# A third seven-product group in the second layer's feed-forward part of a two-layer decoder trunk, with its weight-sum transfers placed in the first layer

## The chip, the cores and the metric

The kernel runs on one core of a Trainium2 chip. The metric is the time of one execution on the device in microseconds (us); of several executions the median is given. About 0.2% (1.6 us) is what a measurement of this kernel can tell from no change.

## The reference, cut to what matters

Two layers work on 256 tokens of 1024 features. Each ends with a SwiGLU feed-forward part, and the change concerns these two parts alone:

```python
D_MODEL = 1024; SEQ = 256
D_FF = 2816                       # ((8 * 1024 + 767) // 768) * 256
...
def swiglu(h, w_gu, w_down):
    g, u = jnp.split(h @ w_gu, 2, axis=-1)
    return (jax.nn.silu(g) * u) @ w_down
...
for l in range(DEPTH):            # DEPTH = 2
    ...                           # layer 0: gated convolution; layer 1: attention; both: memory attention
    x = x + swiglu(rms_norm(x, norm_ffn[l]), ffn_w_gu[l], ffn_w_down[l])
```

All inputs and outputs are float32.

## The kernel before, in words

**Products in two parts.** Every weight matrix streams from DRAM in chunks of 128 x 1024 floats (512 KB). `load_chunk` brings a chunk into a buffer `raw_...` with a DMA on the queue of SyncE (SP). ScalarE (ACT) rounds it into `hi_...` (`split_high`, a CAST), and VectorE (DVE) puts the remainder raw - hi into `lo_...` (`split_low`, a TENSOR_TENSOR). TensorE (PE) adds three products for each pair of parts (`mm3`), and the first of the three takes the lo part. So a weight is usable only when DMA, cast and subtraction are all done, in this order. There are five raw buffers (`RAWS`) and ten pairs of hi and lo (`WBUFS`): the DMA of chunk n can start only when the subtraction of chunk n - 5 is done.

**The feed-forward part** (`swiglu`). The 2816 hidden columns make eleven pairs `jp` of 256 columns. Pairs 0 and 1 are done in another way (`gate_up_rows`). An ordinary pair has two halves of 128 columns: `gate_up` multiplies the gate weights `wg` and the up weights `wu` into two PSUM tiles `gu`; ScalarE copies each out to `gu_sb` (COPY), VectorE adds, ScalarE applies SiLU (ACTIVATE), VectorE multiplies, and the product goes as hi and lo into `guT`. After each half stand two blocks of the down projection of the pair `jp - 2` (`down`, weights `wd`, accumulators `ff`). An ordinary pair with its down blocks streams six chunks: two `wg`, two `wu` and two `wd`.

**A group of seven products** (`seven`, `GROUPS`) replaces the gate and up products of two adjacent pairs jp and jp + 1. The tokens and features are cut in two halves each, the weights into four quarters B11, B12, B21, B22, and seven products (B11, B21, T1, T4, T2, B22, T3) of sums stand for eight. Three of them take quarters of the weights, four take sums of weights T1 to T4. The sums of activations (S1 to S4) are made on VectorE by `token_sums` at the start of the part, once for all groups of a layer. A group streams 14 chunks of weights and four of `wd`, 18 in all where two ordinary pairs stream 12, and it ends with eight transposes (`turn_parts4`, tile `pt_g`) on TensorE. Between the products stand eight down blocks.

**The sums of weights** are made by DMA alone, DRAM to DRAM (`sum_steps`): for each of T1 to T4 and each of two halves, a plain copy on SP's queue, and an adding transfer of another quarter on GpSimd's (POOL's) queue, 16 transfers of 512 KB for a group. T2 is begun from the finished T1, and T4 from the finished T2. `SUMS_AT` says by which chunk's load each transfer is issued: a hook at position n runs just before chunk n of the whole stream is loaded. Positions 64 to 135 are the chunks of the first layer's feed-forward part, 200 to 277 those of the second's.

**What sets the order.** The program is recorded in the order in which the Python code runs. A model clock (`Clock`, `note`) stands behind it: `Feed.pump`, polled after each matmul, issues the cast of the next chunk when the model says that the raw chunk has landed and ScalarE is free, and the subtraction likewise; `Feed.take` forces them at the latest when a product needs them. The model charges 1587 ns for a load, 1460 ns for a copy of `sum_steps` and 3300 ns for an adding transfer, one after the other. On the chip each engine then runs its instructions in just that order, whatever the time is.

The profile's line L464 is the matmul, L468 the transpose, L242 any VectorE or ScalarE operation, L481 a load, L553 and L551 a copy and an adding transfer of `sum_steps`. The first layer has one group, at pair 8, and the second layer two, at pairs 4 and 8.

Of the kernel before, what the change touches and what calls it, by code (L numbers as in the profile page):

```python
# [42 lines left out]
SPARE = 1500  # L43
LATER = 2000
BANKWISE = 5
GROUPS = ((8,), (4, 8))
SUMS_AT = ((44, 104, 104), (128, 220, 210))


class Rows:  # L50
# [18 lines left out]
def weight_plan():  # L69
# [38 lines left out]
    def seven_plan(l, jp):  # L108
        plan = []
        for name in SEVEN:  # L110
            if name[:4] == "down":
                plan += down_plan(l, jp - ROW_PAIRS + int(name[4]))
                continue
            for i in range(2):
                it = dict(name=f"w{name}_{l}_{jp}_{i}", a=2, b=2 * T, gain=None, pieces=1, halves=1)
                if name[0] == "T":
                    it["sum"] = l, jp, name, i
                else:
                    kh, part = QUARTER[name]
                    k, c = 4 * kh + 2 * i, part * DFF + jp * T  # L120
                    it["src"] = ffn_w_gu[l][k * P:(k + 2) * P, c:c + 2 * T]
                plan.append(it)
        return plan
# [7 lines left out]
    def ffn_plan(l):  # L131
        steps, last = ffn_steps()
        plan = []
        for kind, jp in steps + [("down", jp) for jp in last]:
            if kind == "gu" and jp in GROUPS[l]:
                plan += seven_plan(l, jp)
            elif kind == "gu" and jp - 1 in GROUPS[l] or kind == "down" and \
                    any(jp + ROW_PAIRS - g in (0, 1) for g in GROUPS[l]):
                pass
# [32 lines left out]
    for l in range(2):  # L172
        for jp in GROUPS[l]:
            for name in QUARTER:
# [224 lines left out]
def yoco_kernel(  # L399
# [22 lines left out]
    vector, scalar, pool = (Timed(clock, n, e) for n, e in  # L422
                            (("dve", nc.vector), ("act", nc.scalar), ("pool", nc.gpsimd)))
    side = Side(clock, tp=2, gu=2, half=HALVES, pair=PAIRS)
# [8 lines left out]
    def tp_tile(name):  # L433
        return ps_tp.tile([P, 4, P], F32, tag="tp", name=name)
# [21 lines left out]
    def tok(h):  # L456
        return slice(h * P, (h + 1) * P)
# [9 lines left out]
    def transpose(o, i):  # L467
        nc.tensor.transpose(o, i, ident[:i.shape[0], :i.shape[0]])  # L468
        clock.note("pe", 109, [o], [i], 200)
# [65 lines left out]
    def sum_steps(l, jp):  # L535
        for name in ("T1", "T2", "T3", "T4"):
            for i in range(2):
                weight_sums[l, jp, name, i] = aside.tile([P, 2, 2 * T], F32, name=f"{name}_{l}_{jp}_{i}")

        def step(name, source, i, add):  # L540
            dst = weight_sums[l, jp, name, i]
            if source[0] == "T":
                src = weight_sums[l, jp, source, i]
            else:
                n = quarters[l, jp, source, i]
                src = chunks[n * P:(n + 1) * P].rearrange("p (a n) -> p a n", a=2)

            def run():
                clock.free["dma"] = max(clock.free["dma"], clock.now)
                if add:  # L550
                    nc.gpsimd.dma_start(dst, src, accum_op=OP.add, max_dma_last_dim=2048)  # L551
                else:
                    nc.sync.dma_start(dst, src)  # L553
                clock.note("dma", 3300 if add else 1460, [], [])

            return run

        order = (("T1", "B11", False), ("T3", "B12", False), ("T1", "B12", True), ("T3", "B22", True),
                 ("T2", "T1", False), ("T2", "B22", True), ("T4", "T2", False), ("T4", "B21", True))
        return [step(name, source, i, add) for name, source, add in order for i in range(2)]  # L560

    plan, _, quarters, ffn_steps = weight_plan()
    feed = side.feed = Feed(clock, plan, load_chunk, split_high, split_low)
# [71 lines left out]
    def split_steps(hi, lo, pt, kind="tp"):  # L635
        scalar.copy(hi, pt)
        yield
        vector.tensor_sub(lo, pt, hi)
        side.give(kind)
        yield  # L640
# [398 lines left out]
        feed.hooks[36 + k] = [put_aside(k)]  # L1039

    for l in range(2):
        steps = [step for jp in GROUPS[l] for step in sum_steps(l, jp)]
        first, end, last = SUMS_AT[l]
        for n, step in enumerate(steps):
            at = min(first + (end - first) * n // len(steps), last + n - len(steps))
            feed.hooks.setdefault(at, []).append(step)


    def short_conv(act, into):
# [179 lines left out]
    def swiglu(l, src, done, fine_end=False, at_end=None):  # L1229
        act = src.act  # L1230
        guT = Act(side, [])

        def unit_of(j):
            if j // 4 == len(guT.units):
                guT.units.append(acts.tile([P, 4, 2, T], F32R, tag="unit", name=f"guT{l}_{j // 4}"))
            return guT.units[j // 4], j % 4
# [121 lines left out]
        def seven(jp):  # L1358

            u, j0 = unit_of(2 * jp)  # L1360
            bank_jobs, t = {}, {}
# [60 lines left out]
            def b22(acc):  # L1422
                side.finish(bank_jobs["T2"])
                yield from new("u0")
                vector.tensor_add(t["u0"], acc, t["m1"])
                side.give("gu")
                t["w used"] = True
                yield
                side.finish(bank_jobs["B21"])
                vector.tensor_mul(t["u0"], t["u0"], t["g0"])  # L1430
                side.give("half")
                yield spare(jp)
                yield from turn_parts4(t["u0"], 0)

            def t3(acc):
                while not t.get("w used"):
                    yield 0
                vector.tensor_add(t["m1"], acc, t["m1"])
                side.give("gu")
                yield  # L1440
                side.finish(bank_jobs["T4"])
                vector.tensor_sub(t["p5"], t["p5"], t["m1"])
                yield
                scalar.activation(t["p5"], t["p5"], AF.Silu)
                yield
                vector.tensor_mul(t["p5"], t["p5"], t["m1"])
                side.give("half")
                yield spare(jp)
                yield from turn_parts4(t["p5"], 1)
# [5 lines left out]
            def turn_parts4(src, h):  # L1455
                yield from side.hold("tp")
                pt = tp_tile("pt_g")
                for i in range(4):
                    transpose(pt[:, i, :], src[:, i * P:(i + 1) * P])
                side.give("half")  # L1460
                yield
                yield from split_steps(u[:, :, 0, tok(h)], u[:, :, 1, tok(h)], pt)

            EVICT = {"B11": b11, "B21": b21, "T1": t1, "T3": t3, "T2": t2, "B22": b22, "T4": t4}
            n = jp - ROW_PAIRS
# [17 lines left out]
                next_down()  # L1483
            next_down()
            for h, name in enumerate(("B22", "T3")):
                guT.add_job(h, jp // 2, bank_jobs[name])

        def down_w(jp):
            return [feed.take(f"wd{l}_{2 * jp + i}") for i in range(2)]
# [14 lines left out]
        steps, last = ffn_steps()  # L1504
        sums_job = [side.start(token_sums())]
        for jp in range(ROW_PAIRS, NP):
            if jp in GROUPS[l]:
                seven(jp)
            if jp in GROUPS[l] or jp - 1 in GROUPS[l]:
                continue  # L1510
            w = gu_w(jp)
            n = jp - ROW_PAIRS
            gate_up(jp, w, 0)
            wd = down_w(n) if ("down", n) in steps else None
            for h in range(2):
                if h == 1:
                    gate_up(jp, w, 1)
                for b in range(2 if wd else 0):
                    if h == b == 1:
                        feed.free(2)  # L1520
                    down(n, wd, h, b)
# [239 lines left out]
```

## Time and profile before

| | |
|---|---|
| median of three runs | 783.81 us (783.09 to 784.54) |
| the profiled execution, time | 783.19 us |
| its span, first to last instruction | 781.4 us |
| granted TensorE clock | 0.998 |
| TensorE busy | 773.5 us, 99% of the span |
| VectorE, ScalarE busy | 574.0 us (73%), 459.0 us (59%) |
| first layer's feed-forward part, on TensorE | 200.7 to 378.3 us |
| second layer's feed-forward part, on TensorE | 594.6 to 775.2 us |

The profiled execution lies 0.6 us under the median, inside the spread of the three runs. A busy TensorE is matmul after matmul without a pause; where it has to wait for a weight, the waiting shows as a hole between two of its rows. Each engine runs in order, so an instruction that waits holds back all that stand behind it.

### The profile page before, as it was taken

How to read it: one execution, taken by the hardware profiler on the slowest of the kernel's cores; microseconds unless marked ns; L12 is line 12 of the kernel's file. 1: busy time of each engine (PE TensorE's matmuls, PEld its weight loads, DVE VectorE, ACT ScalarE, POOL GpSimd, SP SyncE). 2: the span in 40 equal slices, each digit the busy share in tenths (PEclk: the TensorE clock that was granted, in tenths of full speed). 3: DMA queues.
4: the chain of work that ended last, by engine and by line, in shares of the span. 5: the costliest groups of instructions: out<-in, count | busy, mean ns of one | idle time of the engine just before them, and what ended most of it. 6: DMA issues, size and time to landing. Idle time of an engine off the chain costs nothing.

```text
span 781.4 us, 11230 instructions
## 1 busy us (share of the span) xinstructions
PE 773.5 (99%) x4147; PEld 664.8 (85%) x4147; DVE 574.0 (73%) x872; ACT 459.0 (59%) x728; POOL 39.1 (5%) x68
## 2 busy tenths in 40 slices
PE   9999999999999999999999999999999999999996
PEld 8988888898888888888888889888988888888885
DVE  6988887768785566688756566876867876966964
ACT  7875666665654555566654563655756556655741
POOL 1000011000100000000100010020001000000000
PEclk9999999999999999999999999999999999999999
DMA  9876888926676755699788466889975646946921
GB/s 343 299 259 212 272 292 267 336 65 212 188 247 235 223 177 204 206 367 346 211 251 295 178 161 210 302 239 300 247 209 166 240 159 216 330 165 210 348 107 54
DMA packets 53415, 182.71 MB, mean 234 GB/s; under 512 B 6256, under 2 KB 7280, under 8 KB 52720
## 3 DMA queue, kind: packets, MB, share of 16 engines
q1 hardware_dynamic: 45968, 166.79, 60.0%
q0 software_dynamic: 6816, 14.68, 10.4%
q8 instruction: 32, 0.52, 0.3%
q10 hardware_dynamic: 576, 0.52, 0.2%
q14 instruction: 23, 0.19, 0.1%
HBM read 178.82 MB, written 28.31 MB: 265 GB/s over the span
## 4 chain that ended last, share of the span: by engine, by line
PE 98%; DVE 1%; issue 0%; ACT 0%; POOLq 0%; DVEq 0%; ACTq 0%
PE gu L464 17%; PE ff L464 15%; PE seven L464 7%; PE acc_memk L464 6%; PE q_acc L464 6%; PE cu L464 6%; PE rows L464 6%; PE acc_mo L464 6%; PE acc_memv L464 6%; PE pb L464 3%; PE acc_v L464 3%; PE acc_q L464 3%; PE acc_o L464 3%; PE acc_cout L464 3%; PE acc_k L464 3%; PE po L464 2%
## 5 line engine op out<-in xcount | busy, mean ns | idle before, releaser
L464 PE MATMUL ff<-hi_wd,guT 128*128 128x512 f32 (+1 forms) x352 | 108.3, 388 | 0.0
L464 PEld LDWEIGHTS ff<-hi_wd,guT 128*128 128x128 f32 x352 | 65.8, 188 | 12.8
L464 PE MATMUL ff<-lo_wd,guT 128*128 128x512 f32 (+1 forms) x176 | 68.3, 388 | 0.0
L242 DVE TENSOR_TENSOR gu_sb<-gu_sb,gu 128x256 f32<-128x256 f32 x48 | 19.9, 420 | 57.5 <-ACT gu_sb L242 57.0
L242 DVE TENSOR_TENSOR lo_wd<-raw_wd,hi_wd 128x1024 fp32r<-128x1024 f32 x44 | 53.4, 1219 | 3.7 <-ACT hi_wd L242 3.6
L242 ACT COPY gu_sb<-gu 128x256 f32<-128x256 f32 x48 | 17.8, 373 | 60.0 <-PE gu L464 59.6
L242 ACT CAST hi_wd<-raw_wd 128x1024 fp32r<-128x1024 f32 x44 | 46.1, 1050 | 11.3 <-DMA raw_wd<-in_chunks_dram 11.0
L464 PE MATMUL gu<-ffn,hi_wg 128*128 128x512 f32 x192 | 48.0, 390 | 0.0
L464 PE MATMUL gu<-ffn,hi_wu 128*128 128x512 f32 x192 | 47.6, 390 | 0.0
L464 PE MATMUL acc_memk<-mT,hi_memk 128*128 128x256 f32 x256 | 44.3, 291 | 0.0
L242 ACT CAST hi_wu<-raw_wu 128x1024 fp32r<-128x1024 f32 x32 | 33.6, 1052 | 17.3 <-DMA raw_wu<-in_chunks_dram 12.6
L464 PEld LDWEIGHTS gu<-ffn,hi_wg 128*128 128x128 f32 x192 | 35.9, 188 | 7.3
L464 PEld LDWEIGHTS gu<-ffn,hi_wu 128*128 128x128 f32 x192 | 35.8, 188 | 7.3
L464 PE MATMUL rows<-hi_wr,ffn 128*128 128x512 f32 x128 | 40.7, 395 | 0.0
L464 PE MATMUL acc_mo<-hi_mo,oT_mem 128*128 128x512 f32 x128 | 40.6, 393 | 0.0
L242 DVE TENSOR_TENSOR lo_wu<-raw_wu,hi_wu 128x1024 fp32r<-128x1024 f32 x32 | 38.8, 1219 | 1.3 <-ACT hi_wu L242 1.2
L464 PE MATMUL acc_memv<-hi_memv,mT 128*128 128x512 f32 x128 | 39.6, 390 | 0.0
L464 PEld LDWEIGHTS acc_memk<-mT,hi_memk 128*128 128x128 f32 x256 | 38.7, 197 | 0.6 <-ACT hi_memk L242 0.4
L464 PEld LDWEIGHTS ff<-lo_wd,guT 128*128 128x128 f32 x176 | 33.2, 188 | 6.3
L551 POOL DMA_DIRECT2D T<-in_chunks_dram x24 | 21.9, 913 | 271.4 <-issue 92.1
L242 POOL TENSOR_TENSOR rs<-ms,neg_half 128x1 f32<-128x1 f32 x14 | 13.4, 960 | 395.5 <-DVE ms L242 386.3
L464 PE MATMUL q_acc<-mem,hi_mq 128*128 128x512 f32 x128 | 32.4, 394 | 0.0
(277 smaller groups left out, 1963.8 us busy)
## 6 DMA issues: line engine op xcount, KB each, us to landing
raw_wd<-in_chunks_dram SPq DMA_DIRECT2D x44, 512.0 KB, 5.1
raw_wu<-in_chunks_dram SPq DMA_DIRECT2D x32, 512.0 KB, 5.0
T<-in_chunks_dram POOLq DMA_DIRECT2D x24, 512.0 KB, 8.6
raw_wg<-in_chunks_dram SPq DMA_DIRECT2D x24, 512.0 KB, 5.2
raw_wT<-T SPq DMA_DIRECT2D x24, 512.0 KB, 4.8
raw_wB<-in_chunks_dram SPq DMA_DIRECT2D x18, 512.0 KB, 4.8
raw_memv<-in_chunks_dram SPq DMA_DIRECT2D x16, 512.0 KB, 5.0
raw_mq<-in_chunks_dram SPq DMA_DIRECT2D x16, 512.0 KB, 5.1
```

What stands on the lines that cost most here:

```text
L242: return call(out, *args, **kw)
L464: nc.tensor.matmul(o, l, r, start=start, stop=stop)
L551: nc.gpsimd.dma_start(dst, src, accum_op=OP.add, max_dma_last_dim=2048)
```

## The change

The second layer's groups stand at pairs 3, 6 and 8 instead of 4 and 8, so that six pairs instead of four are done by seven products. The sixteen transfers of the new set of sums, for pair 3, stand at positions 94 to 116, in the first layer's feed-forward part. The 48 other transfers keep their positions: the sixteen at 128 to 171 now make the sums for pair 6. Since pair 3 begins in the middle of a tile of `guT`, its result is written in two parts of 128 x 256 to two tiles, and its two jobs are registered for both.

```diff
-GROUPS = ((8,), (4, 8))
-SUMS_AT = ((44, 104, 104), (128, 220, 210))
+GROUPS = ((8,), (3, 6, 8))
+SUMS_AT = {
+    (0, 8): (44, 47, 51, 55, 59, 62, 66, 70, 74, 77, 81, 85, 89, 92, 96, 100),
+    (1, 3): (94, 95, 97, 98, 100, 101, 107, 108, 103, 104, 106, 107, 111, 112, 115, 116),
+    (1, 6): (128, 130, 133, 136, 139, 142, 145, 148, 151, 153, 156, 159, 162, 165, 168, 171),
+    (1, 8): (174, 176, 179, 182, 185, 188, 191, 194, 197, 199, 202, 205, 206, 207, 208, 209),
+}
...
     for l in range(2):
-        steps = [step for jp in GROUPS[l] for step in sum_steps(l, jp)]
-        first, end, last = SUMS_AT[l]
-        for n, step in enumerate(steps):
-            at = min(first + (end - first) * n // len(steps), last + n - len(steps))
-            feed.hooks.setdefault(at, []).append(step)
+        for jp in GROUPS[l]:
+            for at, step in zip(SUMS_AT[l, jp], sum_steps(l, jp)):
+                feed.hooks.setdefault(at, []).append(step)
...
-                yield from split_steps(u[:, :, 0, tok(h)], u[:, :, 1, tok(h)], pt)
+                if j0 == 0:
+                    yield from split_steps(u[:, :, 0, tok(h)], u[:, :, 1, tok(h)], pt)
+                    return
+                for i, v in enumerate((u, unit_of(2 * jp + 2)[0])):
+                    c, q = slice(2 - 2 * i, 4 - 2 * i), pt[:, 2 * i:2 * i + 2, :]
+                    scalar.copy(v[:, c, 0, tok(h)], q)
+                    yield
+                    vector.tensor_sub(v[:, c, 1, tok(h)], q, v[:, c, 0, tok(h)])
+                side.give("tp")
+                yield
...
             for h, name in enumerate(("B22", "T3")):
-                guT.add_job(h, jp // 2, bank_jobs[name])
+                for g in sorted({jp // 2, (jp + 1) // 2}):
+                    guT.add_job(h, g, bank_jobs[name])
```

The rows below show how three stretches of the program stand before and after. In a name, the number after the kind is the layer (0 is the first), then come the pair and the chunk: `hi_wd0_9` is the hi part of chunk 9 of the first layer's down weights, `hi_wT1_0_8_1` that of the second half of sum T1 for pair 8.

First, the queue of SyncE in the first layer, where the weights of pairs 5 and 6 are loaded. Before:

```order
L481 DMA raw_wu0_5_1_2854<-in_chunks_dram 128x1024
L481 DMA raw_wd0_6_2872<-in_chunks_dram 128x1024
L481 DMA raw_wd0_7_2883<-in_chunks_dram 128x1024
L481 DMA raw_wg0_6_0_2895<-in_chunks_dram 128x1024
L481 DMA raw_wg0_6_1_2907<-in_chunks_dram 128x1024
L481 DMA raw_wu0_6_0_2946<-in_chunks_dram 128x1024
```

In the change:

```order
L486 DMA raw_wu0_5_1_2862<-in_chunks_dram 128x1024
L558 DMA T1_1_3_0_503<-in_chunks_dram 16x8192
L486 DMA raw_wd0_6_2881<-in_chunks_dram 128x1024
L558 DMA T1_1_3_1_504<-in_chunks_dram 16x8192
L486 DMA raw_wd0_7_2893<-in_chunks_dram 128x1024
L486 DMA raw_wg0_6_0_2905<-in_chunks_dram 128x1024
L558 DMA T3_1_3_0_507<-in_chunks_dram 16x8192
L486 DMA raw_wg0_6_1_2918<-in_chunks_dram 128x1024
L558 DMA T3_1_3_1_508<-in_chunks_dram 16x8192
L486 DMA raw_wu0_6_0_2958<-in_chunks_dram 128x1024
```

Four copies for the new group now stand between five loads of weights.

Second, ScalarE in the first layer, around the end of pair 5 and the first half of pair 6. `gu_sb0` and `gu_sb1` are the copies of gate and up out of PSUM; those into `gu_sb0_3090`/`gu_sb1_3091` before, and into `gu_sb0_3098`/`gu_sb1_3099` in the change, belong to the second half of pair 5. Before:

```order
L242 COPY gu_sb0_3090<-gu_3092 128x256
L242 CAST hi_wd0_8_3129<-raw_wd0_8_3022 128x1024
L242 COPY gu_sb1_3091<-gu_3104 128x256
L242 ACTIVATE gu_sb0_3090<-gu_sb0_3090 128x256
L242 CAST hi_wd0_9_3146<-raw_wd0_9_3033 128x1024
L242 CAST guT0_2_2858<-gu_sb1_3091 128x256
L242 CAST hi_wg0_7_0_3165<-raw_wg0_7_0_3044 128x1024
```

In the change:

```order
L247 COPY gu_sb0_3098<-gu_3100 128x256
L247 COPY gu_sb1_3099<-gu_3116 128x256
L247 ACTIVATE gu_sb0_3098<-gu_sb0_3098 128x256
L247 CAST guT0_2_2866<-gu_sb1_3099 128x256
L247 CAST hi_wd0_8_3165<-raw_wd0_8_3035 128x1024
L247 COPY gu_sb0_3169<-gu_3171 128x256
L247 CAST hi_wd0_9_3208<-raw_wd0_9_3044 128x1024
L247 COPY gu_sb1_3170<-gu_3183 128x256
L247 ACTIVATE gu_sb0_3169<-gu_sb0_3169 128x256
L247 CAST hi_wg0_7_0_3224<-raw_wg0_7_0_3061 128x1024
```

The cast of `wd0_9` has moved from pair 5 to behind the first copy of pair 6 (`gu_sb0_3169`). The down blocks that take `wd0_8` and `wd0_9` are the ones right after that half of pair 6, as before. One pair later `hi_wd0_11` has moved in the same way, from behind the SiLU of pair 6 to behind the second copy, `gu_sb1`, of pair 7's first half.

Third, ScalarE at the first layer's group (pair 8). `m1`, `p5` and `g0` are made from the products B11, T1 and B21. Before:

```order
L242 CAST hi_wB21_0_8_1_3443<-raw_wB21_0_8_1_3330 128x1024
L242 CAST guT0_3_3157<-gu_sb1_3388 128x256
L242 CAST hi_wT1_0_8_0_3460<-raw_wT1_0_8_0_3341 128x1024
L242 CAST hi_wT1_0_8_1_3470<-raw_wT1_0_8_1_3353 128x1024
L242 CAST hi_wT4_0_8_0_3481<-raw_wT4_0_8_0_3392 128x1024
L242 COPY m1_3484<-seven_3455 128x512
L242 CAST hi_wT4_0_8_1_3501<-raw_wT4_0_8_1_3450 128x1024
```

In the change:

```order
L247 COPY m1_3487<-seven_3467 128x512
L247 CAST hi_wB21_0_8_1_3497<-raw_wB21_0_8_1_3403 128x1024
L247 CAST hi_wT1_0_8_0_3509<-raw_wT1_0_8_0_3417 128x1024
L247 ACTIVATE g0_3523<-g0_3523 128x512
L247 CAST hi_wT1_0_8_1_3539<-raw_wT1_0_8_1_3461 128x1024
L247 COPY p5_3551<-seven_3532 128x512
L247 CAST hi_wT4_0_8_0_3560<-raw_wT4_0_8_0_3475 128x1024
L247 CAST hi_wT4_0_8_1_3568<-raw_wT4_0_8_1_3493 128x1024
```

Before, four casts stood ahead of the copy out of the first product; in the change each of them stands behind the result of the product just ahead of it. The order of TensorE's products in the first layer is unchanged; some transposes between them stand a few products later.

## The prediction

> **What bounds the kernel now.** I read the page first, then the chain of waits in both feed-forward parts, then the order of time on ScalarE, VectorE, SyncE and GpSimd around the two places that the change touches. The page says which engine sets the time:
>
> ```profile
> PE 773.5 (99%) x4147; PEld 664.8 (85%) x4147; DVE 574.0 (73%) x872; ACT 459.0 (59%) x728; POOL 39.1 (5%) x68
> ...
> PE 98%; DVE 1%; issue 0%; ACT 0%; POOLq 0%; DVEq 0%; ACTq 0%
> ```
>
> TensorE is busy for 99% of the span and makes 98% of the chain that ended last. So work taken from TensorE is worth its full length, and a hole in TensorE costs its full length too: nothing later gives it back. Two questions follow. What do fewer products save, and do the weights still come in time for each product?
>
> **What the new group saves.** The chain in the second layer, start and length in us, shows an ordinary pair (two halves of 5.54 and two double down blocks of 2.75), then the group at pair 4, then the next ordinary pair with the group's last transposes in it:
>
> ```profile
> 635.07 5.54 PE gu L464 x32
> 640.61 2.75 PE ff L464 x12
> 643.36 5.54 PE gu L464 x32
> 648.90 2.75 PE ff L464 x12
> 651.65 2.72 PE seven L464 x12
> ...
> 679.74 2.76 PE ff L464 x12
> 682.50 1.59 PE gu L464 x7
> 684.09 0.44 PE pt_g L468 x4
> 684.52 4.00 PE gu L464 x25
> ```
>
> A pair lasts 651.65 - 635.07 = 16.58, two of them 33.16. The group lasts 682.50 - 651.65 = 30.85, and its last four transposes, 0.44, fall into the next pair: 31.29. One more group in place of two pairs saves 33.16 - 31.29 = 1.9 us of TensorE.
>
> The group needs more of the others: 18 chunks instead of 12. A stretch of 32.87 us over the first group shows what that takes; in the row each engine has its busy time and instructions:
>
> ```profile
> 651.65:684.52 32.87, 32.87 (x148) 26.88 (x148) 30.54 (x33) 22.57 (x25) 0.00 (x0) 1.00 0.91 314
> ```
>
> TensorE (first) is busy all of it, VectorE (third) for 30.54, 93%, with DMA at 0.91. Groups at pairs 6 and 8 now follow each other without an ordinary pair between. That still fits: 93% twice is 93%, and it leaves 2.3 us a group. No lead is needed to pay for it, so I take nothing; if VectorE lost all of that margin once, 2.3 us would be gone. Below zero it can't go, as nothing of it was waited for. Pair 3 in two parts costs ScalarE and VectorE two short instructions each for each of two halves, in the same margin: nothing. Starting one pair earlier, at about 635 instead of 651.65, asks for the activation sums by the third product, about 643; they are done well ahead of that, and their cover is 13 us:
>
> ```profile
> 628.65 1.28 DVE L242 TENSOR_TENSOR S<-S,S 128x512 fp32r<-128x512 f32 x2
> ```
>
> **What the sixteen transfers cost.** They go out in the first layer, between the loads of pairs 5 to 8. Their own work is DMA; the same 60 us of before show the room there (last two numbers: DMA share, GB/s):
>
> ```profile
> 258.00:318.00 60.00, 60.00 (x318) 51.89 (x317) 37.73 (x52) 30.07 (x50) 0.00 (x0) 1.00 0.63 212
> ```
>
> A share of 0.37 of 60 us is free, 22 us. 212 GB/s at a share of 0.63 make 336 at a full one, and sixteen transfers of 512 KB, 8.4 MB, would take 25 us at that rate. So loads come some us later, which is not yet a hole, as long as chunks lie ready ahead of their use. The 48 other transfers keep their positions; nothing for them.
>
> The price comes by another way, which the order shows. The recording charges the transfers on its model clock and so sees weights land later; it puts casts further back in ScalarE's queue, behind copies out of PSUM that wait for TensorE. On the chip the cast can't run ahead of such a copy, even when its data lie there. I walk along the changed order with the durations of before. First TensorE's chain in the first layer:
>
> ```profile
> 296.39 2.75 PE ff L464 x12
> ...
> 312.97 2.75 PE ff L464 x12
> ...
> 324.00 2.72 PE seven L464 x12
> 326.72 1.36 PE ff L464 x6
> 328.08 2.72 PE seven L464 x12
> 330.80 1.37 PE ff L464 x6
> 332.17 2.80 PE seven L464 x12
> 334.97 1.39 PE ff L464 x6
> 336.36 2.73 PE seven L464 x12
> 339.09 1.37 PE ff L464 x6
> 340.45 2.80 PE seven L464 x12
> 343.25 1.39 PE ff L464 x6
> ```
>
> Then ScalarE: the cast that moves (`hi_wd`, before at 289.04), the copies behind which casts now stand, and a SiLU:
>
> ```profile
> 289.04 1.05 ACT L242 CAST hi_wd<-raw_wd 128x1024 fp32r<-128x1024 f32 x1
> ...
> 295.52 0.37 ACT L242 COPY gu_sb<-gu 128x256 f32<-128x256 f32 x1 [0.24 <-PE gu L464]
> ...
> 313.06 0.37 ACT L242 COPY gu_sb<-gu 128x256 f32<-128x256 f32 x1 [0.59 <-PE gu L464]
> ...
> 326.76 0.59 ACT L242 COPY m<-seven 128x512 f32<-128x512 f32 x1 [0.37 <-PE seven L464]
> ...
> 334.49 0.63 ACT L242 ACTIVATE g<-g 128x512 f32<-128x512 f32 x1
> ```
>
> And VectorE's subtraction of a chunk and its addition behind a product:
>
> ```profile
> 291.20 1.22 DVE L242 TENSOR_TENSOR lo_wd<-raw_wd,hi_wd 128x1024 fp32r<-128x1024 f32 x1
> ...
> 332.16 0.68 DVE L242 TENSOR_TENSOR g<-seven,m 128x512 f32<-128x512 f32 x1
> ```
>
> All times below are on the clock of before, each wait worked out as if those ahead of it had only shifted everything.
>
> 1. `wd0_9`, pair 6: copy 295.52 + 0.37, cast 1.05, subtraction 1.22, usable at 298.16. The down blocks begin at 296.39 and want it after a quarter of 2.75, at 297.08: a hole of 1.1. Before, it was usable from 292.42 (291.20 + 1.22).
> 2. `wd0_11`, pair 7: second copy 313.06 + 0.37 + 1.05 + 1.22 = 315.70; wanted at 312.97 + 0.69 = 313.66: 2.0.
> 3. Second half of B21, behind the copy of B11: 326.76 + 0.59 + 1.05 + 1.22 = 329.62; wanted at 328.08 + 1.36 = 329.44: 0.2.
> 4. Second half of T1, behind the SiLU on B21: B21 ends at 330.80 + 0.2; addition 0.68, SiLU 0.63, cast 1.05, subtraction 1.22: 334.58. Wanted at 332.17 + 0.2 + 1.40 = 333.77: 0.8.
> 5. First half of T4, behind the copy of T1: T1 ends 334.58 + 1.40 = 335.98; copy 0.59, cast 1.05, subtraction 1.22: 338.84. Wanted after 1.39 of down blocks, at 337.37: 1.5.
> 6. First half of B22: here the five raw buffers decide. Its load may start when the second half of T4 is subtracted, 338.84 + 1.22 = 340.06. The loads' time to land, from the page, with the adding transfers' below it:
>
> ```profile
> raw_wd<-in_chunks_dram SPq DMA_DIRECT2D x44, 512.0 KB, 5.1
> ...
> T<-in_chunks_dram POOLq DMA_DIRECT2D x24, 512.0 KB, 8.6
> ```
>
> Landed at 345.2, cast 346.2; on VectorE stand one more subtraction and an addition ahead (to 346.9), so usable at 348.1. TensorE comes there at 338.84 + 2.73 + 1.37 + 2.80 + 1.39 = 347.1: 1.0. After this the gaps between evictions are wide enough again.
>
> The Trainium skill ("DMA: Bandwidth & Descriptors", anatomy of one DMA) fits a transfer on GpSimd's path as 2.0 us plus bytes over 436 GB/s, by which an estimate for 512 KB is 3.2 us. By that figure item 6 would vanish and the sum be 1.0 less; the page's rows of this case, 5.1 and 8.6, decide here.
>
> Sum of holes: 1.1 + 2.0 + 0.2 + 0.8 + 1.5 + 1.0 = 6.6. Bounds: at the low end only items 1 and 2, where the casts demonstrably stand behind a copy and nothing but row durations enters, 3.1; if landing grows from 5.1 to the 8.6 of the adding transfers, item 6 and those after it grow by 3.5 to about 10.
>
> Net: -1.9 + 6.6 = +4.7. The profiled execution, 783.19 (span 781.4), becomes 787.9; the median of three is 0.6 higher, so I say 788.5 for a median.
>
> GpSimd's queue: its adding transfers follow each other at some 9.9 us where they queue, and the last one of the old set goes out just as the new copies start:
>
> ```profile
> 256.89 0.90 POOL L551 DMA_DIRECT2D T<-in_chunks_dram x1 [7.60 <-issue]
> ...
> 380.19 0.56 POOL L242 TENSOR_TENSOR rs<-ms,neg_half 128x1 f32<-128x1 f32 x1 [21.37 <-DVE ms L242]
> ...
> 531.02 0.94 POOL L551 DMA_DIRECT2D T<-in_chunks_dram x1 [8.34 <-issue]
> 540.96 0.89 POOL L551 DMA_DIRECT2D T<-in_chunks_dram x1 [8.99 <-issue]
> ```
>
> Five more at 9.9 put the start of T2's second half at 306.4 and its landing at 315.0. The copy for T4's second half waits for that on SyncE, ahead of the loads of B21 for the group. B21's own raw buffer comes free only with item 2's subtraction, 315.7 plus the 1.1 of item 1, so this wait hides behind it, with 1.8 us to spare. The eighth starts at 336.1, far ahead of the normalization factor that GpSimd makes at 380.19 (the row with `rs`); nothing.
>
> **The rivals.**
>
> - *The wait on SyncE shows.* If adding transfers among the denser loads take 10 to 11 us each and follow at 11.7, the fifth starts at 256.9 + 5 x 11.7 = 315.4 and lands near 326. SyncE holds B21's load until then, 9 us after its buffer is free; the group begins with weights 4 to 5 us later still. Against it stands 9.9 as measured under such load; for it, the share of 0.63 before anything is added. Holes 6.6 + 4.5: 783.8 - 1.9 + 11.1 = 793.0.
> - *Everything is hidden.* Casts move but TensorE has enough work before it. The Trainium skill ("Perfetto Trace Analysis", Identifying the Most-Contended Engine) says to optimize the engine of highest occupancy first, and by this rule only TensorE's work would count. The row for it: 99% busy, so 783.8 - 1.9 = 781.9. Against it: in items 1 and 2 the cast stands behind a copy of a tile that TensorE finishes a quarter of a block before it wants the weight.
> - *Only the ordinary pairs stall.* Items 1 and 2 happen, the delay lets the loads catch up, and the group runs free: 783.8 - 1.9 + 3.1 = 785.0.
>
> **How the numbers follow.** I give my forecast 0.60, the SyncE wait 0.16, the two-item case 0.12, the hidden one 0.12. About 0.2%, 1.6 us, is what can be told from no change: 785.0 lies inside it, 781.9 just outside on the fast side, the other two on the slow side. So faster 0.12, same 0.12, slower 0.76. The forecast's own range is 786.5 to 791; to hold 8 in 10 the range goes from the two-item case, 784.8, to the SyncE wait, 793.0, leaving out the hidden case and the tails.
>
> **What would show it.** Right: in the first layer TensorE's chain has holes of about 1 and 2 us inside the first down blocks of pairs 6 and 7, released by `lo_wd` on VectorE, and of 0.2 to 1.5 inside the group; VectorE's waits for casts, and casts directly behind copies on ScalarE. The first layer's feed-forward part takes 6 to 7 us longer, and the second layer's part 1.9 less, without holes. Wrong: an unbroken chain in the first layer (then the hidden rival), SyncE standing at a copy of T4 for over 5 us (then the first rival), or holes in the second layer's consecutive groups.

## The result, and the profile after

The changed kernel takes 789.97 us (median of 5 runs, 789.87 to 792.04), the kernel before 783.38 on the same chip. The ratio is 1.009 with an interval of 1.0074 to 1.0106: slower by 6.6 us. The profiled execution is 789.87 with a span of 788.1 (before 783.19 and 781.4), so the two traces can be laid beside each other. First the page, engines and the chain that ended last:

```profile
PE 773.2 (98%) x4111; PEld 660.8 (84%) x4111; DVE 582.3 (74%) x875; ACT 463.8 (59%) x726; POOL 45.7 (6%) x76
...
PE 91%; DMA 2%; DVE 2%; ACT 1%; issue 1%; POOLq 0%; DVEq 0%; ACTq 0%
```

TensorE has 36 matmuls less to do and still the span is longer, and the chain, which before was on TensorE for 98% of its length, is on it for 91%. Where it leaves is told by TensorE's waits (total, times, longest, in us). Of these, the kernel before had none in either feed-forward part:

```profile
PE ff L469 <- DVE lo_wd L247: 3.1, 2, 2.0
PE seven L469 <- DVE lo_wT L247: 2.4, 2, 1.5
...
PE seven L469 <- DVE lo_wB L247: 0.7, 2, 0.5
PE pt_g L473 <- DVE u L247: 0.5, 1, 0.5
```

The first three rows are six waits in the first layer, two for down weights, two for sums, two for quarters. The fourth is in the second layer. The chain in the first layer shows the first two at their place, with ScalarE and VectorE in between (start, length):

```profile
290.98 4.59 PE gu L469 x24
...
295.66 0.37 ACT gu_sb L247
296.03 0.96 ACT hi_wd L247
...
297.01 1.24 DVE lo_wd L247
...
298.29 2.33 PE ff L469 x9
300.62 5.54 PE gu L469 x32
...
314.54 0.37 ACT gu_sb L247
314.91 0.95 ACT hi_wd L247
315.89 1.24 DVE lo_wd L247
...
317.18 2.34 PE ff L469 x9
319.51 5.54 PE gu L469 x32
```

It is copy, cast, subtraction, matmul, as the order said. The same places in the kernel before, and behind them the first block after the group and the projection after the feed-forward part:

```profile
299.14 5.54 PE gu L464 x32
...
315.71 5.54 PE gu L464 x32
...
354.85 1.82 PE gu L464 x8
...
386.28 10.92 PE acc_k L464 x48
```

In the change the last two are these:

```profile
362.86 2.05 PE gu L469 x10
...
394.01 10.94 PE acc_k L469 x48
```

So the block of 299.14 begins at 300.62, the one of 315.71 at 319.51, the one of 354.85 at 362.86, and the projection of 386.28 at 394.01: the first layer costs 7.7 us.

In the second layer the chain breaks once, in group 3:

```profile
659.00 6.76 DMA raw_wu<-in_chunks_dram
...
665.86 1.06 ACT hi_wu L247
...
666.94 0.04 DVE lo_wu L247
...
668.09 0.69 DVE u L247
668.80 0.70 DVE u L247
...
669.55 0.66 PE pt_g L473 x4
```

The subtraction of a late `wu` chunk stands ahead of the two steps that make `u`, and the group's transposes wait for `u`. The two groups that follow each other have no hole: TensorE's waits list none there. From the first matmul of `rows`, with which the feed-forward part begins, to the last row of gate-and-up products the second layer takes 161.92 us, before 163.05: 1.13 saved. In sum 7.73 - 1.13 = 6.6.

### The profile page after: what moved, and what is told of

It reads as the page before. It is cut to its first block, busy times and chain, and to the rows that moved or that the text cites. A ratio compares the mean times of both kernels' runs of the same rounds, so it can differ in the third digit from the quotient of the medians.

```text
span 788.1 us, 11207 instructions
## 1 busy us (share of the span) xinstructions
PE 773.2 (98%) x4111; PEld 660.8 (84%) x4111; DVE 582.3 (74%) x875; ACT 463.8 (59%) x726; POOL 45.7 (6%) x76
## 4 chain that ended last, share of the span: by engine, by line
PE 91%; DMA 2%; DVE 2%; ACT 1%; issue 1%; POOLq 0%; DVEq 0%; ACTq 0%
PE gu L469 14%; PE ff L469 13%; PE seven L469 7%; PE q_acc L469 6%; PE cu L469 6%; PE rows L469 6%; PE acc_mo L469 6%; PE acc_memv L469 6%; PE acc_memk L469 4%; PE pb L469 3%; PE acc_v L469 3%; PE acc_k L469 3%; PE acc_q L469 3%; PE acc_cout L469 3%; PE acc_o L469 3%; PE po L469 2%
## 5 line engine op out<-in xcount | busy, mean ns | idle before, releaser
L247 DVE TENSOR_TENSOR gu_sb<-gu_sb,gu 128x256 f32<-128x256 f32 x40 | 16.5, 419 | 46.0 <-ACT gu_sb L247 45.8
L247 ACT COPY gu_sb<-gu 128x256 f32<-128x256 f32 x40 | 14.9, 374 | 56.7 <-PE gu L469 56.6
L556 POOL DMA_DIRECT2D T<-in_chunks_dram x32 | 29.1, 909 | 276.1 <-issue 139.8
L247 DVE TENSOR_TENSOR lo_wT<-raw_wT,hi_wT 128x1024 fp32r<-128x1024 f32 x32 | 38.1, 1220 | 6.9 <-ACT hi_wT L247 6.9
L469 PE MATMUL gu<-ffn,hi_wg 128*128 128x512 f32 x160 | 39.9, 390 | 0.0
L469 PE MATMUL gu<-ffn,hi_wu 128*128 128x512 f32 x160 | 39.6, 390 | 0.0
L247 ACT CAST hi_wT<-raw_wT 128x1024 fp32r<-128x1024 f32 x32 | 32.8, 1051 | 11.4 <-DMA raw_wT<-T 9.6
L247 ACT CAST hi_wu<-raw_wu 128x1024 fp32r<-128x1024 f32 x28 | 29.3, 1051 | 10.8 <-DMA raw_wu<-in_chunks_dram 6.5
L469 PEld LDWEIGHTS gu<-ffn,hi_wg 128*128 128x128 f32 x160 | 29.8, 188 | 6.1
L469 PEld LDWEIGHTS gu<-ffn,hi_wu 128*128 128x128 f32 x160 | 29.8, 188 | 6.0
```

What stands on the lines that cost most here:

```text
L247: return call(out, *args, **kw)
L469: nc.tensor.matmul(o, l, r, start=start, stop=stop)
```

## The experiments

All times are medians against the kernel before on the same chip, 783.34 to 783.48.

| run | us (lowest to highest) | ratio, 95% interval |
|---|---|---|
| charge, no transfers, no third group | 792.58 (792.05 to 794.79) | 1.0123 (1.0110 to 1.0136) |
| transfers and charge, no third group | 792.77 (791.95 to 793.10) | 1.0118 (1.0102 to 1.0133) |
| transfers, no charge, no third group | 787.55 (786.36 to 788.70) | 1.0052 (1.0040 to 1.0064) |
| the same, copies not waiting for additions | 784.72 (783.71 to 790.39) | 1.0029 (1.0013 to 1.0045) |
| third group, no charge | 785.98 (785.06 to 788.23) | 1.0033 (1.0020 to 1.0046) |
| groups 4, 6, 8, no charge | 785.46 (784.04 to 787.69) | 1.0032 (1.0019 to 1.0044) |
| third group, half the charge | 783.72 (780.99 to 789.36) | 1.0007 (0.9987 to 1.0027) |
| third group, transfers elsewhere, charged | 787.88 (786.87 to 789.54) | 1.0058 (1.0046 to 1.0070) |
| third group, transfers elsewhere, no charge | 783.12 (782.84 to 784.38) | 0.9996 (0.9988 to 1.0005) |
| third group, last eight moved again, no charge | 781.99 (781.44 to 782.40) | 0.9982 (0.9974 to 0.9991) |

**The charge without a transfer.** My theory says that the order of the recording costs the time; the rival says that the sixteen transfers do. To the kernel before I add only the charge on the model clock, at the sixteen positions:

```diff
+    def charge(add):
+        def run():
+            clock.free["dma"] = max(clock.free["dma"], clock.now)
+            clock.note("dma", 3300 if add else 1460, [], [])
+        return run
+
+    for n, at in enumerate((94, 95, 97, 98, 100, 101, 107, 108, 103, 104, 106, 107, 111, 112, 115, 116)):
+        feed.hooks.setdefault(at, []).append(charge(n // 2 in (2, 3, 5, 7)))
```

> The kernel before, with no transfer added and no third group: only the model clock is charged 1460 or 3300 ns sixteen times, at the sixteen places. Theory A: the first layer's casts take the changed kernel's places, and its 7.7 us of holes come without one byte more being moved: 783.4 + 7.7 = 791.1 us; at the least the six holes that TensorE's waits list, 6.2, so 789.6 to 791.5. Rival B: nothing is transferred, so 783.4 us, within 0.3.

It takes 792.58, 9.2 us more, with no byte more moved (182.71 MB, as before). TensorE's waits are those of the changed kernel, to 0.1 us:

```profile
PE ff L464 <- DVE lo_wd L242: 3.1, 2, 2.0
PE seven L464 <- DVE lo_wT L242: 2.3, 2, 1.5
...
PE seven L464 <- DVE lo_wB L242: 0.7, 2, 0.5
```

So the order alone is enough for all six holes. It is 1.5 us above the 791.1 expected, and the last section shows from which rows that comes.

**The transfers without the charge.** The opposite half: the sixteen transfers are issued, reading weights of pair 4 into sums that nothing reads, and the clock isn't charged for them, so that every cast and matmul stands where it stood before. Of the edit, the part that leaves out the charge:

```diff
-                clock.free["dma"] = max(clock.free["dma"], clock.now)
...
-                clock.note("dma", 3300 if add else 1460, [], [])
+                if (l, jp) != (1, 3):
+                    clock.free["dma"] = max(clock.free["dma"], clock.now)
+                    clock.note("dma", 3300 if add else 1460, [], [])
```

> The kernel before with its two groups, plus sixteen transfers of the same sizes, kinds and queues at the same places, whose sums nothing reads, and which the model clock is not charged for; every cast, matmul and load stands where it stood. Theory A: the transfers lie beside other work, 783.4 us, at most 784.0. Rival B: 789 to 791 us, with TensorE waiting for the first layer's feed-forward weights and the weights for their raw loads or for SyncE.

Neither theory has it: 787.55, 4.2 more. The transfers are not free either. TensorE waits in two stages:

```profile
PE pt_g L468 <- DVE u L242: 2.0, 1, 2.0
PE gu L464 <- DVE gu_sb L242: 1.7, 2, 1.3
```

For the second row, SyncE's queue in this run, where the row of `T<-T` at 289.85 is a copy of a sum that waits for GpSimd's addition, and `raw_wu`, recorded behind it, goes out at 290.44 instead of 283.36:

```profile
281.76 0.53 SPq L481 DMA_DIRECT2D raw_wg<-in_chunks_dram  x1
289.85 0.48 SPq L552 DMA_DIRECT2D T<-T  x1
290.44 1.56 SPq L481 DMA_DIRECT2D raw_wu<-in_chunks_dram  x2
```

And ScalarE, where the casts of this chunk come ahead of the copies out of PSUM, as in the kernel before:

```profile
297.21 1.05 ACT L242 CAST hi_wu<-raw_wu 128x1024 fp32r<-128x1024 f32 x1 [4.26 <-DMA raw_wu<-in_chunks_dram]
299.25 1.05 ACT L242 CAST hi_wu<-raw_wu 128x1024 fp32r<-128x1024 f32 x1 [1.00 <-DMA raw_wu<-in_chunks_dram]
300.21 0.64 ACT L242 COPY gu_sb<-gu 128x256 f32<-128x256 f32 x2
```

ScalarE stands at a cast whose load is late, and the copies that would free PSUM for TensorE stand behind it. That is the same queue with the roles turned round.

The first row, the longest hole of this run, lies in the group, and its chain begins at SyncE too. The copy for T4 waits 4.2 us for an addition, the loads of B21 go out behind it, and from there the loads stay late until `u`:

```profile
307.94 6.39 DMA T<-in_chunks_dram
...
314.35 0.47 SPq L552
...
315.54 9.50 DMA raw_wB<-in_chunks_dram
...
353.52 0.66 PE pt_g L468 x4
```

This is the copy that the prediction's first rival named.

**SyncE's wait, or the traffic?** The four copies from sum to sum read a weight of the same size instead, so they wait for no addition:

```diff
-            if source[0] == "T":
+            if source[0] == "T" and (l, jp) != (1, 3):
                 src = weight_sums[l, jp, source, i]
             else:
-                n = quarters[l, jp, source, i]
+                n = quarters[l, jp, "B11" if source[0] == "T" else source, i]
```

> As the run that has only the sixteen transfers (787.55 us, 4.2 over the kernel before), but the four copies of one sum to another read a weight instead, of the same size and on the same queue, so that they no longer wait on SyncE's queue for GpSimd's additions (the sums are read by nothing there). Theory C (SyncE held by the copy that waits for an addition, raw_wu's load 6.5 us late behind it): the 4.2 us go, 783.4 to 784.4 us, and hi_wu in the first layer does not wait for its load. Theory D (the traffic itself, a DMA share of 0.97 to 1.01 in the stretches from 260 to 380 us): the loads stay slow, 787 us or more. Between 785 and 787 both take part.

It takes 784.72, between the two expectations: by the medians 3.0 of the 4.2 us were SyncE's wait and 1.2 remain with the same bytes. By the ratios (1.0052 and 1.0029, whose intervals touch) it is 1.8 and 2.3, so both take part, and their shares are known no better than this. In this run `raw_wu` goes out at 285.62, and on ScalarE stand its second cast and the copies:

```profile
297.33 1.05 ACT L242 CAST hi_wu<-raw_wu 128x1024 fp32r<-128x1024 f32 x1 [3.68 <-DMA raw_wu<-in_chunks_dram]
298.28 0.64 ACT L242 COPY gu_sb<-gu 128x256 f32<-128x256 f32 x2
```

The load goes out 4.8 us earlier than with the chained copies, the second cast still waits 3.68 us for its data, and the copies out of PSUM come 1.9 us earlier. In this trace that is early enough: TensorE doesn't wait for them. What remains lies elsewhere, 0.3 us of waiting for `u` in the group and 0.9 behind the group, where the chain runs over a load of `raw_k` that takes 8.65 us.

**Both, without the third group.** Here the charge and the transfers are added to the kernel before:

> The kernel before with its two groups, the sixteen transfers at the changed kernel's places and the charge for them: the first layer of the changed kernel without its third group. The charge alone gave 792.58, the transfers alone 787.55. Theory E (the two losses overlap, because a cast placed late no longer needs an early load): 791 us, that is the changed kernel's 789.97 plus the 1.1 us that its second layer saves, between 790.5 and 792.6. Rival (they add up): 783.4 + 9.2 + 4.2 = 796.8 us.

792.77, as much as the charge alone (792.58) and just above the 792.6 that I had set as the upper end. The losses overlap wholly: a cast that stands behind a copy anyway doesn't miss a load that comes a few us late. That the sum would be 796.8 is refuted.

**The changed kernel without the charge.** All of the change but the charge for the sixteen (the diff above, in the changed kernel):

> The changed kernel with all three groups and all sixteen new transfers, but the recording's model clock is not charged for the sixteen transfers, so that the casts of the first layer stand in ScalarE's queue as they do in the kernel before. Theory A (the cost is the casts' new places behind the PSUM copies): the 7.7 us of holes in the first layer go and the 1.1 us that the second layer saved in the changed kernel stays, 783.4 - 1.1 = 782.3 us, between 781.3 and 783.0. Rival B (the cost is the transfers' own traffic, or SyncE's and GpSimd's waits): the transfers are all there, so 789 to 790 us as the changed kernel, TensorE waiting for lo_wd, lo_wT and lo_wB in the first layer.

785.98, 4 us below the changed kernel, but not 782.3. It is the two halves again: 783.4 + 4.2 for the transfers - 1.8 saved in the second layer = 785.8. The same stretch of the second layer takes 161.23 us here, 1.82 less than before, and loses nothing in group 3.

**Three groups in a row, 4, 6 and 8.** Only the place of the third group differs from the run above.

```diff
-GROUPS = ((8,), (3, 6, 8))
+GROUPS = ((8,), (4, 6, 8))
```

> As the run without the charge, but the third group stands at pair 4, so that the three groups (4, 6, 8) follow one another and no ordinary pair stands between them. It asks where 0.8 us of the forecast saving of 1.9 us in the second layer went. Theory A1 (the loss belongs to the place: behind group 3 an ordinary pair's weights come late): the full saving, 783.4 - 1.9 = 781.5 us, and no wait of the second layer's transposes for u. Theory A2 (a third group always loses it, VectorE being 93% busy in a group): 782.3 us as the run without the charge, with a wait of some 0.5 us in one of the groups. Rival B (the transfers cost): 788 us or more for both.

785.46, not to be told from the run above by these intervals; my 781.5 forgot the transfers' cost as the run above did. The second layer takes 161.21 us in its trace. So neither A1 nor A2 holds: a third group doesn't always lose 0.7 us, nor does its place at pair 3 make it lose them.

**Half the charge.** The charge for the sixteen is multiplied by 0.5.

> The changed kernel, transfers at the changed kernel's places, with half the charge (730 and 1650 ns). Theory A with C and D (an order that reckons late loads a little too early leaves casts waiting for loads, one that reckons them late leaves casts behind the PSUM copies, and the two losses overlap): between the run without charge and the changed kernel, 786 to 790 us. Rival (a middle order meets the real landings): below 785 us, both kinds of holes gone.

Inconclusive. The median lies in the rival's range, but the runs spread from 780.99 to 789.36, on both sides. The profiled one is the slowest of them, and its trace says nothing of the others. In it SyncE stands 8.3 us at the copy for T4, the loads of sums behind it land in 6.7 to 9.9 us, and TensorE waits in the group. The lowest is the lowest of all runs here; what parts them stays open.

**The transfers in other places.** If late loads and late casts are all, the third group should pay where queues have room.

```diff
-    (1, 3): (94, 95, 97, 98, 100, 101, 107, 108, 103, 104, 106, 107, 111, 112, 115, 116),
+    (1, 3): (64, 65, 66, 67, 68, 69, 70, 71, 129, 132, 135, 138, 147, 150, 154, 157),
```

> The changed kernel with its three groups; the model clock is not charged for the third group's sixteen transfers, and they stand elsewhere: the first eight at the loads from 64 to 71 (from 156 us on, where the DMA share is 0.43 between 160 and 200 us), the last eight between 129 and 157 among the second group's. Casts and matmuls of the first layer stand as in the kernel before. Theory A (a third group is worth 1.8 us once its transfers find free queues; rows to the last gate and up product took 161.2 us in the run without the charge, 163.05 in the kernel before): 783.4 - 1.8 = 781.6 us, and no new wait of TensorE. Rival (wherever sixteen more transfers go, they delay loads by as much): 785 to 786 us as in the run without the charge.

783.12, no difference from before and 1.5 above the 781.6 expected. The feed-forward part of the first layer is as before up to its last group (the next block at 355.00, before 354.85, and the part had begun 0.18 later), and the second layer's stretch takes 161.18. But the last eight transfers fell in a stretch that is busy already, and the chain loses 1.7 us behind the group (the projection at 388.17, before 386.28):

```profile
360.76 9.67 DMA raw_k<-in_chunks_dram
...
373.35 0.41 ACT guT L247
```

With the charge for these sixteen, at the same places:

> The transfers where the run before has them, but charged on the model clock, as the changed kernel does. It asks whether the charge does harm wherever it stands. Theory A (the casts go behind PSUM copies wherever the model queue is full): slower than the run without the charge by 1 to 5 us, 782.6 to 786.6 us. Rival A' (only at the feed-forward's eight-matmul slots does the order bite; where the model queue has room a charge changes little): 781.6 us, within 0.5.

787.88, 4.8 more for nothing but the charge, and more than the 786.6 that I had set as the upper end. The waits are in the stages between the two layers now, where the last eight are charged:

```profile
PE acc_v L469 <- DVE lo_v L247: 2.4, 2, 1.9
...
PE acc_mo L469 <- DVE oT_mem L247: 1.1, 1, 1.1
```

And without it, the last eight at 165, 166, 167, 168, 174, 175, 176, 177, where the share of DMA was low:

> As the run with the transfers elsewhere (783.12 us), but only its last eight are moved once more: there they stood at 340 to 420 us, where the kernel before already has a DMA share of 0.80 to 0.94, raw_k took 9.7 us to land, and the first gate-and-up product's end to acc_k was 1.9 us longer; here they stand at loads 165 to 177, from 430 us on, where the share is 0.43 to 0.50 between 440 and 480 us. Casts and matmuls stand as in that run. Theory A (two places with free queues, and the whole 1.8 us of the second layer stays): 781.6 us, between 781.2 and 782.4. Rival (the late loads only move to another stage): 783 us, with a wait of 1 to 2 us in the stages after 430 us.

781.99, ratio 0.9982 (0.9974 to 0.9991): 1.35 us less than the kernel before and 8 less than the changed one. The interval leaves out 1, but 1.35 us is less than the 1.6 that I hold for distinguishable. TensorE's waits have nothing left of the two feed-forward parts; these are all:

```profile
PE warm L469 <- DVE blank L769: 1.5, 1, 1.5
PE acc_memk L469 <- DVE lo_memk L247: 0.7, 1, 0.7
```

The second layer's stretch takes 161.20, 1.85 less; 0.6 of it is lost before that stretch begins (`rows` at 595.05, before 594.42).

## Why the prediction was right

The size and its sign came out, 788.5 said and 789.97 measured, and the mechanism is the one forecast. Point by point:

- **The group's saving, 1.9.** As the worth of a group this holds: 1.82, 1.84, 1.87 and 1.85 us in the four runs with three groups and no charge. In the changed kernel the term is 1.1. It was mis-sized because I looked at VectorE's share, 93%, and not at what stands ahead in its queue. In the trace `lo_wu`, for a load that took 6.76 us, stands ahead of `u`, and 0.7 us are lost, of which TensorE's wait lists 0.5. The same subtraction stands ahead of `u` in the run without the charge, at the same place, and there no time is lost. So the order alone doesn't do it; why the load was late in this kernel and not in the four others isn't settled.
- **Groups 6 and 8 back to back; pair 3 in two parts; the token sums.** No hole in any of them, as said.
- **The six holes, 6.6.** Items 1 and 2: 1.1 and 2.0 said, 3.1 measured. Items 4 and 5: 2.3 said, 2.4 measured. Items 3 and 6: 1.2 said, 0.7 measured. For item 5 the copy isn't the only cause in the changed kernel: its load lands at 340.75, 0.15 before the cast starts, and the chain that ended last runs over the load. In the run with only the charge the chain runs over the copy, and the hole is as long (1.49 against 1.50). All six waits sum to 6.2. But the layer is 7.7 longer: a hole costs more than its wait. The block behind the first hole starts 1.48 later (0.13 of it was there already, 290.98 against 290.85), where the wait is 1.1; behind the second 2.32 more, where the wait is 2.0. Some 0.25 to 0.3 a hole are not in the wait. In the trace a matmul begins 0.23 behind the one before it and lasts 0.39, so that neighbours overlap by about 0.17; at a hole this overlap is gone, and the first matmul behind it takes 0.50, 0.11 more. Six holes make the 1.5 by which the layer exceeds its waits, and my sum had no term for it.
- **The cause, the model clock's charge.** Shown: the charge alone makes the six holes (792.58), it adds 4.8 us at other places too, and taking it away gives 4 us back.
- **The transfers' own DMA: nothing.** This is right for the changed kernel, where they add nothing to the charge (792.77 against 792.58), and wrong as a statement about the transfers. With the casts where they were they cost 4.2. That the term came out as nothing is luck: another loss covers it. I had the rows for it, a cast in ScalarE's queue that waits for its load and copies behind it, and looked only at casts behind copies; and my own estimate had 25 us of transfers for 22 us of room.
- **The rival with SyncE's wait.** It doesn't decide in the changed kernel: the copy for T4 that I feared goes out at 310.94, and the load of B21 waits for its raw buffer until 317.15. But a copy does hold SyncE, one step earlier than I looked (T2's second half, for 3.3 us until 287.75, with `raw_wu` behind it at 288.32):

```profile
287.75 0.48 SPq L558 DMA_DIRECT2D T<-T  x1
288.32 4.37 SPq L486 DMA_DIRECT2D raw_wu<-in_chunks_dram  x2
```

  Where the charge doesn't cover it, SyncE's waits are worth 2 to 3 us, and there the copy for T4 is one of them: 4.2 us in the trace of the transfers alone and 8.3 in that of half the charge. The rival's mechanism is real; the charge puts it out of sight.
- **The hidden rival, 781.9.** It needs both an order that hasn't moved and transfers that no load meets. 781.99 is what came when both were arranged, though from a kernel before at 783.34: 1.35 saved, where the rival has 1.9.

So -1.9 + 6.6 = +4.7 for the profiled execution was -1.1 + 7.7 = +6.6. Both terms were mis-sized by about 1 us, and to the same side.

## What to carry to other kernels

When a model sets the order in which a kernel is recorded, a transfer has two prices: what it does on the chip and what its charge does to the order. Time them apart, by charging without moving and by moving without charging, before adding them up: here the sum was as small as the larger of the two. An in-order queue that holds both casts of loaded weights and copies out of PSUM can lose either way, so new transfers belong where neither the loads nor the model's queue are late, and a copy that depends on a slow addition belongs far behind it or off the queue that loads the weights. The last two were not tried here; what was tried is a copy that waits for no addition.

## What the runs showed of the hardware

**The same hole, with and without a slower clock behind it.** The second hole is 2.03 us long in the changed kernel and in both runs that have the charge and two groups. Behind it the granted clock was 1.00 in the changed kernel, in the stretch of the hole (row by stretch, the third number from the end is the clock) and in the one after it:

```profile
316.00:320.00 4.00, 2.83 (x12) 2.36 (x13) 2.89 (x5) 2.16 (x4) 0.00 (x0) 1.00 1.00 239
```

and in the run with only the charge:

```profile
316.00:320.00 4.00, 2.99 (x8) 2.37 (x9) 2.90 (x5) 2.17 (x4) 0.00 (x0) 0.67 0.42 133
320.00:324.00 4.00, 4.00 (x18) 3.24 (x17) 1.59 (x2) 1.10 (x2) 0.00 (x0) 0.90 0.53 150
```

There a matmul of 128x512 took 0.63 us instead of 0.39, and the nine of the down block 3.91 instead of 2.34:

```profile
317.01 3.91 PE ff L464 x9
```

That is the 1.5 us by which this run passed its expectation, and it belongs to the clock, not to the waits. In the run with charge and transfers the clock fell to 0.69 at the same place. The Trainium skill ("TensorE: Matmul & The Clock Gate", Part 1) says that the clock is halved after an idle window of about 3.4 us and that this window runs freely. The traces agree that equal holes can end differently, but here 2.0 us of idle time, beside full work, were enough; in the changed kernel without the charge 1.8 us were, with 0.81 and 0.76 behind it. Of the eight holes of 1.8 to 2.6 us in the traces here six were followed by a lower clock, and two, of 1.97 and 2.03 us, were not. So a hole of 2 us on TensorE can cost 3.5. This doesn't explain why the changed kernel's own runs lie at 789.87 to 789.97 and at 791.52 to 792.04: over the whole execution the granted clock was 0.997 in the first three and 0.998 and 0.999 in the two longer ones. What parts them stays open.

**Loads and additions at a fuller DMA share.** In the stretch from 255 to 400 us the changed kernel without the charge moves 42.6 MB, the kernel before 36.1. The median time of a 512 KB load of `wd` from issue to landing grew from 5.6 us to 8.2 (16 loads each). GpSimd's additions, slow already, took 10.0 us before (5 of them) and 9.7 with the new transfers (13).
